# Attention's value product, one head at a time: high and low parts of the values side by side in the columns of the array

## The chip, the cores and the metric

The kernel runs on one core of a Trainium2 chip. The metric is the device time of one execution in microseconds (us). TensorE (PE in the profile; PEld is its loading of weights) multiplies matrices, VectorE (DVE) and ScalarE (ACT) work element by element, GpSimd (POOL) helps out, and SyncE (SP) issues most of the DMAs. Each engine works through its own list in order and waits where an operand or a buffer is not ready.

## What is computed

One decoder layer for 256 positions of width 1024, in float32. Cut to what matters here:

```python
proj = x @ w_in                      # q | k | v | B | C | h | gate_attn | gate_conv
y_att = moba_attention(q, k, v) @ w_attn_out       # 8 heads of 64
y_cnv = (gate_b * causal_dwconv(gate_c * h_in, conv_w_mix)) @ w_conv_out
mix = (g_att * y_att + g_cnv * y_cnv) @ w_o
x = layer_norm(ALPHA * x + mix)
u = causal_dwconv(x @ w_up);  f = (silu(u_gate) * u_val) @ w_down
x = layer_norm(ALPHA * x + f)
```

The block length of the attention is 256, so with 256 positions it is plain causal attention: for each head, `softmax(q k^T / 8, causal) @ v`.

## The kernel before

**High and low parts.** Every float32 factor `a` is split into two numbers of the type that TensorE reads here (F32R): `h`, a copy rounded to it by ScalarE, and `l = a - h`, by VectorE. A product then takes three passes, high by high, high by low and low by high; the fourth, low by low, is left out. `mm3` (lines 305 to 307) writes the three passes one after the other; `hl_split` (219, 220) and `low` (216) make the parts.

**Weights.** They come from memory in chunks of two units (128 x 1024 each), in three raw buffers. `split_h` (192) and `split_l` (197) make `wh` and `wl` of a unit. The DMA that refills a raw buffer waits on SyncE's queue until `split_l` has read what was in it.

**Slots.** After the products for q, k and v the kernel goes through the weight units one after the other; a unit is a slot. C0 is the first unit after q, k and v, and slot n below means unit C0+n. Slots 0 to 11 are the short convolution's products, slots 12 to 27 the 16 gate products (g0 to g15, slot 12+j for gj), and from slot 28 on come the products `y` of the mixed stage, which read the attention's result `aT`. What else is to be done is written into the slots by hand, with `at(slot, part, function)`. In each slot the instructions are issued in this order: the slot's weight product and then its "pe" entries on TensorE; its "act" entries and then `split_h` of the unit 5 slots ahead on ScalarE; `split_l` of the unit 4 slots ahead and then its "dve" entries on VectorE. Entries of one slot stand in the order of registration: attention pair 0 to 3 first, then the convolution, then the gates.

**Gate products.** `cols_pair` issues 8 products 512 wide (323) for each unit and, at the second unit of a pair, 16 products 256 wide (330) for both. Their sum lies in two halves of a PSUM bank; two slots later ScalarE copies one half (639) and VectorE adds the other (643, `gs`). There are four such banks, so product g(j+4) can start only when `gs` number j is done. `gate` (646) is the sigmoid; it stands one slot after its `gs` and reads it.

**Attention, by pairs of heads.** In slots 4 to 13 the scores, the masks and the exponentials are done. What follows for pair p:

- `normalize` (418, 422) on VectorE, `probs_T` (428 to 430) on TensorE: six transposes of 128 x 128 into two PSUM banks, one per head;
- `probs_h` (434) and `probs_l` (216), one slot later for the first head and two slots later for the second: the transposed probabilities' parts, into `PT` (in the profile `vpt`, which holds the values as well);
- `attend`: six products into one PSUM bank, with the values of both heads (128 columns) as weights and both heads' queries side by side in the bank (512 wide for the keys 0 to 127, 256 wide for the keys 128 to 255);
- `attend_h` (451) and `attend_l` (216): from each head's columns in the bank its 64 rows are kept, the rest is dropped, and `aT`'s high and low part are made from them, one head at a time.

The banks of scores, transposes and `attend` come from a pool of four that is used in turn. The slots of these steps are in the last `for` of the diff, as `(masked, exps, normalize, probs_T, attend)` for each pair.

Of the kernel before, what the change touches and what calls it, by code (L numbers as in the profile page):

```python
# [12 lines left out]
AF = mybir.ActivationFunctionType  # L13
ALU = mybir.AluOpType

P = 128
S = 256
# [3 lines left out]
HD = 64  # L21
# [116 lines left out]
def layer_kernel(ctx: ExitStack, tc: tile.TileContext, x, wpack, cpack, ln1_g, ln1_b, ln2_g, ln2_b, out):  # L138
    nc = tc.nc
# [10 lines left out]
    def acc_bank(name):  # L150
        return psum.tile([P, 512], F32, tag="acc", name=name)

    def ps_bank(name):
        return ps_pool.tile([P, 512], F32, tag="ps", name=name)

    def scratch(shape, name, bufs=None, tag="scr"):
        return tmp.tile(shape, F32, tag=tag, name=name, bufs=bufs or 6)
# [57 lines left out]
    def low(l, src, h):  # L215
        nc.vector.tensor_tensor(l, src, h.bitcast(F32), op=ALU.subtract)

    def hl_split(h, l, src, eng=None):
        nc.scalar.activation(h, src, AF.Copy)  # L219
        (eng or nc.vector).tensor_tensor(l, src, h.bitcast(F32), op=ALU.subtract)  # L220
# [82 lines left out]
    def mm3(o, ah, al, bh, bl, start, stop):  # L303

        nc.tensor.matmul(o, ah, bh, start=start, stop=False)  # L305
        nc.tensor.matmul(o, ah, bl, start=False, stop=False)  # L306
        nc.tensor.matmul(o, al, bh, start=False, stop=stop)  # L307
# [34 lines left out]
    qk = big.tile([P, 2, 2, AW], F32, tag="rows", name="qk")  # L342
    qkT = big.tile([P, 2, KT, S], F32R, tag="b16", name="qkT")
    vpt = big.tile([P, 3584], F32R, tag="c16", name="vpt")
    vp = vpt[:, 0:2048].rearrange("p (a t n) -> p a t n", a=2, t=2)
    PT = vpt[:, 2048:3584].rearrange("p (a j n) -> p a j n", a=2, j=2)
    aT = big.tile([P, 4, 2, S], F32R, tag="d8", name="aT")
    yT = big.tile([P, 4, 2, S], F32R, tag="e8", name="yT")
# [30 lines left out]
    SB, SM, PR = {}, {}, {}  # L379
# [58 lines left out]

    def attend(p):

        b = ps_bank(f"av{p}")
        vs = slice(p * P, (p + 1) * P)
        mm3(b, vp[:, 0, 0, vs], vp[:, 1, 0, vs], PT[:, 0, :, 128:384], PT[:, 1, :, 128:384], True, False)
        late = b.rearrange("p (j q) -> p j q", j=2)[:, :, 128:256]
        mm3(late, vp[:, 0, 1, vs], vp[:, 1, 1, vs], PT[:, 0, :, 0:128], PT[:, 1, :, 0:128], False, True)
        PR[p, "o"] = b

    def attend_h(p):
        for j in range(2):
            hs = slice(j * HD, (j + 1) * HD)  # L450
            nc.scalar.activation(aT[hs, p, 0, :], PR[p, "o"][hs, j * 256:(j + 1) * 256], AF.Copy)

    def attend_l(p):
        for j in range(2):
            hs = slice(j * HD, (j + 1) * HD)
            low(aT[hs, p, 1, :], PR[p, "o"][hs, j * 256:(j + 1) * 256], aT[hs, p, 0, :])

# [2 lines left out]
    def at(u, part, f, *a):  # L462
        beside.setdefault(u, {}).setdefault(part, []).append((f, a))
# [29 lines left out]

    def evac_v(banks):
        for t in range(2):
            hl_split(vp[:, 0, t], vp[:, 1, t], banks[t])

    C0 = U[(OFF_H, 0)]
    for t in range(2):
# [5 lines left out]

    at(C0 + 4, "pe", scores, (0, 1))
    at(C0 + 9, "pe", scores, (2, 3))
    for p, (m, e, n, tr, av) in enumerate(((5, 6, 8, 11, 14), (7, 8, 14, 15, 18), (10, 11, 17, 19, 22), (12, 13, 21, 23, 26))):
        at(C0 + m, "dve", masked, p)
        at(C0 + e, "act", exps, p)  # L510
        at(C0 + n, "dve", normalize, p)
        at(C0 + tr, "pe", probs_T, p)
        for j in range(2):
            at(C0 + tr + 1 + j, "act", probs_h, p, j)
            at(C0 + tr + 1 + j, "dve", probs_l, p, j)
        at(C0 + av, "pe", attend, p)
        at(C0 + av + 1, "act", attend_h, p)
        at(C0 + av + 1, "dve", attend_l, p)


    def x_split(k):
# [18 lines left out]
    banks = [[acc_bank(f"{m}{t}") for t in range(2)] for m in "qk"] + [[ps_bank(f"v{t}") for t in range(2)]]  # L540
# [24 lines left out]
    for k in range(1, KT):  # L565
        for m in range(3):
            if k >= KT - 2 and m < 2:
                split(C0 + 2 * (k - KT + 2) + m)
            qkv_passes(k, m, (0, 1), (0, 1, 2))
            if k == KT - 1:  # L570
                if m < 2:
                    evac_rows(m, banks[m])
                else:
                    evac_v(banks[m])
        qkv_split(k + 2)
        if 2 <= k <= 4:
            rope_tables(k - 2)
# [199 lines left out]
    banks = [acc_bank(f"o0{nh}") for nh in range(2)]  # L777
# [6 lines left out]
    banks = [acc_bank(f"o1{nh}") for nh in range(2)]  # L784
# [136 lines left out]
    for c in range(1, NP // 2):  # L921
        for e in range(2):
# [3 lines left out]
            d = i - 3  # L926
# [122 lines left out]
```

## Time and profile before

| what | value |
|---|---|
| time, median of 3 runs | 366.98 us (366.85 to 367.76) |
| profiled execution, its own time | 369.54 us |
| span of the profiled execution | 367.6 us |
| busy, PE / PEld | 357.9 / 309.7 us |
| busy, DVE / ACT / POOL | 296.9 / 222.9 / 12.9 us |
| gate products and attention's second part (slots 12 to 27) | about 80 to 131 us of the span |

Times in the profile are counted from the start of the span. A row of the timeline gives the start, the duration, engine, line, operation, what is written and read, and, in brackets, how long the engine had been idle before and what ended that. A row of the chain of waits gives the start, the time up to the next link and what ran. The durations of products are modelled ends; how fast they follow one another is read from their starts.

### The profile page before, as it was taken

How to read it: one execution, taken by the hardware profiler on the slowest of the kernel's cores; microseconds unless marked ns; L12 is line 12 of the kernel's file. 1: busy time of each engine (PE TensorE's matmuls, PEld its weight loads, DVE VectorE, ACT ScalarE, POOL GpSimd, SP SyncE). 2: the span in 40 equal slices, each digit the busy share in tenths (PEclk: the TensorE clock that was granted, in tenths of full speed). 3: DMA queues.
4: the chain of work that ended last, by engine and by line, in shares of the span. 5: the costliest groups of instructions: out<-in, count | busy, mean ns of one | idle time of the engine just before them, and what ended most of it. 6: DMA issues, size and time to landing. Idle time of an engine off the chain costs nothing.

```text
span 367.6 us, 5212 instructions
## 1 busy us (share of the span) xinstructions
PE 357.9 (97%) x1958; PEld 309.7 (84%) x1958; DVE 296.9 (81%) x510; ACT 222.9 (61%) x380; POOL 12.9 (3%) x34
## 2 busy tenths in 40 slices
PE   7999999999999999999999999999999999999991
PEld 6888888889888888888888888888888888888891
DVE  4795697779887669989769798879778697999784
ACT  4773866666976676654276665756757476686300
POOL 2000000000000002301000000000000000000000
PEclk9999999999999999999999999999999999999998
DMA  8988363524836543597250827356280726662011
GB/s 268 351 305 341 116 231 134 210 114 130 329 123 221 179 166 114 201 335 261 119 211 27 306 111 261 116 229 227 118 339 28 318 77 269 230 233 111 2 57 57
DMA packets 11240, 69.61 MB, mean 189 GB/s; under 512 B 1232, under 2 KB 1616, under 8 KB 4176
## 3 DMA queue, kind: packets, MB, share of 16 engines
q1 hardware_dynamic: 10496, 67.00, 49.3%
q0 software_dynamic: 576, 2.10, 1.8%
q8 instruction: 15, 0.25, 0.3%
q10 hardware_dynamic: 144, 0.20, 0.1%
q14 instruction: 9, 0.07, 0.1%
HBM read 68.24 MB, written 1.05 MB: 189 GB/s over the span
## 4 chain that ended last, share of the span: by engine, by line
PE 96%; DVE 1%; DMA 1%; DVEq 0%; SPq 0%; issue 0%
PE pb L323 20%; PE pb L330 10%; PE g L323 8%; PE d L305 5%; PE d L306 5%; PE d L307 5%; PE g L330 4%; PE y L323 4%; PE q L546 3%; PE k L546 3%; PE v L546 3%; PE b L323 2%; PE y L330 2%; PE c L323 2%; PE o L307 2%; PE h L323 2%
## 5 line engine op out<-in xcount | busy, mean ns | idle before, releaser
L197 DVE TENSOR_TENSOR wl<-raw,wh 128x1024 fp32r<-128x1024 f32 x99 | 121.2, 1226 | 27.2 <-ACT wh L192 26.6
L192 ACT ACTIVATE wh<-raw 128x1024 fp32r<-128x1024 f32 x99 | 103.7, 1054 | 32.5 <-DMA raw<-in_wpack 32.4
L323 PE MATMUL pb<-x1T,wh 128*128 128x512 f32 x320 | 76.2, 390 | 0.0
L323 PEld LDWEIGHTS pb<-x1T,wh 128*128 128x128 f32 x320 | 59.7, 188 | 12.2
L330 PEld LDWEIGHTS pb<-x1T,wl 128*128 128x128 f32 x320 | 41.0, 191 | 1.6
L330 PE MATMUL pb<-x1T,wl 128*128 128x256 f32 x320 | 41.5, 283 | 0.0
L220 DVE TENSOR_TENSOR wl<-raw,wh 128x1024 fp32r<-128x1024 f32 (+1 forms) x29 | 27.2, 982 | 9.6 <-ACT wh L219 9.3
L323 PE MATMUL g<-xT,wh 128*128 128x512 f32 x128 | 31.7, 394 | 0.0
L305 PE MATMUL d<-wh,f 128*128 128x512 f32 x80 | 31.3, 391 | 0.0
L306 PE MATMUL d<-wl,f 128*128 128x512 f32 x80 | 31.3, 391 | 0.0
L307 PE MATMUL d<-wh,f 128*128 128x512 f32 x80 | 31.1, 389 | 0.0
L219 ACT ACTIVATE wh<-raw 128x1024 fp32r<-128x1024 f32 (+1 forms) x29 | 23.7, 859 | 10.4 <-DMA raw<-in_wpack 6.2
L323 PEld LDWEIGHTS g<-xT,wh 128*128 128x128 f32 x128 | 23.2, 188 | 4.4
L835 DVE SCALAR_TENSOR_TENSOR fc<-fb,consts,fc 128x254 f32<-128x254 f32 x40 | 19.3, 483 | 1.4
L827 ACT ACTIVATE fc<-fb,consts 128x256 f32<-128x256 f32 x40 | 18.0, 497 | 2.0 <-DVE fb L821 2.0
L833 DVE SCALAR_TENSOR_TENSOR fc<-fb,consts,fc 128x255 f32<-128x255 f32 x40 | 19.1, 478 | 0.0
L817 ACT ACTIVATE fb<-pb 128x512 f32<-128x512 f32 x20 | 11.8, 591 | 9.8 <-PE pb L330 9.8
L307 PEld LDWEIGHTS d<-wh,f 128*128 128x128 f32 x80 | 15.0, 188 | 3.2
L305 PEld LDWEIGHTS d<-wh,f 128*128 128x128 f32 x80 | 15.1, 189 | 2.7
L306 PEld LDWEIGHTS d<-wl,f 128*128 128x128 f32 x80 | 15.1, 188 | 2.6
L330 PEld LDWEIGHTS g<-xT,wl 128*128 128x128 f32 x128 | 16.4, 191 | 0.6
L330 PE MATMUL g<-xT,wl 128*128 128x256 f32 x128 | 16.6, 283 | 0.0
(181 smaller groups left out, 577.7 us busy)
## 6 DMA issues: line engine op xcount, KB each, us to landing
raw<-in_wpack SPq DMA_DIRECT2D x55, 1024.0 KB, 5.0
raw<-in_wpack SPq DMA_DIRECT2D x6, 896.0 KB, 5.7
xr<-in_x SPq DMA_DIRECT2D x1, 1024.0 KB, 7.1
ln<-in_ln_g POOLq DMA_DIRECT2D x2, 512.0 KB, 5.3
ln<-in_ln_b POOLq DMA_DIRECT2D x2, 512.0 KB, 5.9
raw<-in_wpack SPq DMA_DIRECT2D x3, 256.0 KB, 3.8
raw<-in_wpack SPq DMA_DIRECT2D x1, 512.0 KB, 5.9
out<-x SPq DMA_DIRECT2D x2, 256.0 KB, 2.0
```

What stands on the lines that cost most here:

```text
L192: nc.scalar.activation(units[u]["h"], raw_of(u), AF.Copy)
L197: nc.vector.tensor_tensor(units[u]["l"], raw_of(u), units[u]["h"].bitcast(F32), op=ALU.subtract)
L219: nc.scalar.activation(h, src, AF.Copy)
L220: (eng or nc.vector).tensor_tensor(l, src, h.bitcast(F32), op=ALU.subtract)
L305: nc.tensor.matmul(o, ah, bh, start=start, stop=False)
L306: nc.tensor.matmul(o, ah, bl, start=False, stop=False)
L307: nc.tensor.matmul(o, al, bh, start=False, stop=stop)
L323: nc.tensor.matmul(bank, un["h"][:, k, n0:n0 + P], b[:, k].rearrange("p a s -> p (a s)"), start=k == 0, stop=False)
L330: nc.tensor.matmul(bank[:, 0:S], un["l"][:, k, n0:n0 + P], b[:, k, 0], start=False, stop=k == nk - 1)
L546: nc.tensor.matmul(banks[m][t], (xl if p == 2 else xh)[:, k, t * P:(t + 1) * P], wl if p == 1 else wh, start=k == 0 and p == 0, stop=k == ...
L833: nc.vector.scalar_tensor_tensor(c[:, 1:S], pb[:, a * S:a * S + S - 1], w_ffn(1, j), c[:, 1:S], op0=ALU.mult, op1=ALU.add)
L835: nc.vector.scalar_tensor_tensor(c[:, 2:S], pb[:, a * S:a * S + S - 2], w_ffn(0, j), c[:, 2:S], op0=ALU.mult, op1=ALU.add)
```

## The change

The values `vp` are laid out anew: for each pair of heads 256 columns, namely the first head's high and low part and the second head's low and high part, 64 columns each. `attend` now takes one head at a time: its weights are the 128 columns of that head (high and low part), and the moving operand is the high and the low part of that head's probabilities side by side (2 x 256 queries for the keys 0 to 127, 2 x 128 for the rest). So there are four products per pair in place of six, in two PSUM banks in place of one. Each bank holds all four cross products of its head in separate corners, and three of them must be added: `attend_out` copies two corners to SBUF with ScalarE (four copies of 64 rows per pair) and adds them on GpSimd, `attend_sum` adds the third on VectorE out of PSUM, and `attend_hl` splits the sum into `aT`'s two parts. The second step of the split on ScalarE thus comes behind `split_h` of its slot and behind VectorE's sum. Pairs 2 and 3 have some slots moved one earlier.

```diff
-    vp = vpt[:, 0:2048].rearrange("p (a t n) -> p a t n", a=2, t=2)
+    vp = vpt[:, 0:2048].rearrange("p (t g n) -> p t g n", t=2, g=4)
...
     def attend(p):
-        b = ps_bank(f"av{p}")
-        vs = slice(p * P, (p + 1) * P)
-        mm3(b, vp[:, 0, 0, vs], vp[:, 1, 0, vs], PT[:, 0, :, 128:384], PT[:, 1, :, 128:384], True, False)
-        late = b.rearrange("p (j q) -> p j q", j=2)[:, :, 128:256]
-        mm3(late, vp[:, 0, 1, vs], vp[:, 1, 1, vs], PT[:, 0, :, 0:128], PT[:, 1, :, 0:128], False, True)
-        PR[p, "o"] = b
-
-    def attend_h(p):
+        PR[p, "o"] = [ps_bank(f"av{p}_{j}") for j in range(2)]
+        for j in range(2):
+            b = PR[p, "o"][j]
+            js = slice(j * P, (j + 1) * P)
+            nc.tensor.matmul(b, vp[:, 0, p, js], PT[:, :, j, 128:384], start=True, stop=False)
+            nc.tensor.matmul(b.rearrange("p (a q) -> p a q", a=2)[:, :, 128:256], vp[:, 1, p, js], PT[:, :, j, 0:128],
+                             start=False, stop=True)
+
+    def attend_out(p):
+        c = PR[p, "c"] = scratch([P, 2, S], f"ac{p}")
+        for j in range(2):
+            b, hs, ls = PR[p, "o"][j], slice(j * HD, (j + 1) * HD), slice((1 - j) * HD, (2 - j) * HD)
+            nc.scalar.activation(c[hs, 0], b[hs, S:2 * S], AF.Copy)
+            nc.scalar.activation(c[hs, 1], b[ls, 0:S], AF.Copy)
+        nc.gpsimd.tensor_tensor(c[:, 0], c[:, 0], c[:, 1], op=ALU.add)
+
+    def attend_sum(p):
+        c = PR[p, "c"]
         for j in range(2):
             hs = slice(j * HD, (j + 1) * HD)
-            nc.scalar.activation(aT[hs, p, 0, :], PR[p, "o"][hs, j * 256:(j + 1) * 256], AF.Copy)
-
-    def attend_l(p):
-        for j in range(2):
-            hs = slice(j * HD, (j + 1) * HD)
-            low(aT[hs, p, 1, :], PR[p, "o"][hs, j * 256:(j + 1) * 256], aT[hs, p, 0, :])
+            nc.vector.tensor_tensor(c[hs, 0], PR[p, "o"][j][hs, 0:S], c[hs, 0], op=ALU.add)
+
+    def attend_hl(p):
+        hl_split(aT[:, p, 0, :], aT[:, p, 1, :], PR[p, "c"][:, 0])
...
     def evac_v(banks):
         for t in range(2):
-            hl_split(vp[:, 0, t], vp[:, 1, t], banks[t])
+            b = banks[t].rearrange("p (g j d) -> p g j d", g=4, j=2)
+            o = vp[:, t].rearrange("p g (a d) -> p g a d", d=HD)
+            hl_split(o[:, :, 0:4:3], o[:, :, 1:3], b)
...
-    for p, (m, e, n, tr, av) in enumerate(((5, 6, 8, 11, 14), (7, 8, 14, 15, 18), (10, 11, 17, 19, 22), (12, 13, 21, 23, 26))):
+    for p, (m, e, n, tr, av) in enumerate(((5, 6, 8, 11, 14), (7, 8, 14, 15, 18), (10, 11, 17, 18, 21), (12, 13, 20, 22, 25))):
...
         at(C0 + av, "pe", attend, p)
-        at(C0 + av + 1, "act", attend_h, p)
-        at(C0 + av + 1, "dve", attend_l, p)
+        at(C0 + av + 1, "act", attend_out, p)
+        at(C0 + av + 2, "dve", attend_sum, p)
+        at(C0 + av + 2, "dve", attend_hl, p)
```

## The prediction

> **What bounds the kernel now.** I read the busy times first, then the shares of the chain that ended last, then that chain in order of time from 40 us on, where the attention lies.
>
> ```profile
> PE 357.9 (97%) x1958; PEld 309.7 (84%) x1958; DVE 296.9 (81%) x510; ACT 222.9 (61%) x380; POOL 12.9 (3%) x34
> ...
> PE 96%; DVE 1%; DMA 1%; DVEq 0%; SPq 0%; issue 0%
> ...
> 87.16 0.23 PE av L305
> 87.39 0.23 PE av L306
> 87.61 0.23 PE av L307
> 87.84 0.11 PE av L305
> 87.95 0.12 PE av L306
> 88.07 0.12 PE av L307
> 88.19 1.84 PE g L323 x8
> ...
> 98.19 1.84 PE g L323 x8
> ...
> 111.03 1.84 PE g L323 x8
> ...
> 130.53 0.93 PE y L323 x4
> ...
> 131.93 0.93 PE y L323 x4
> ```
>
> TensorE carries 96% of the chain, and between the rows shown here link follows link with no other engine between them. So a product less is time less, as long as no new wait opens on TensorE, and a new wait counts in full. How near VectorE and ScalarE are to opening one, the busy times of the stage tell (columns: stretch, length, then PE, PEld, DVE, ACT, POOL busy, clock, DMA):
>
> ```profile
> 80.00:105.00 25.00, 25.00 (x149) 22.14 (x148) 22.82 (x51) 19.35 (x40) 0.00 (x0) 1.00 0.51 184
> 105.00:131.00 26.00, 26.00 (x154) 23.02 (x153) 18.56 (x32) 19.02 (x36) 0.00 (x0) 1.00 0.52 188
> ```
>
> From 80 to 105 us VectorE is busy for 22.82 of 25 us. There is little room for more work, and none for waiting.
>
> **What TensorE saves.** The six products of a pair take 88.19 - 87.16 = 1.03 us, 0.23 for one 512 wide and 0.115 for one 256 wide. Two of each are left: 0.69. The four pairs save 4 x 0.34 = 1.37 us. That is the whole possible gain; it would bring 366.98 to 365.6.
>
> **What the others pay.** The rows of slots 15 to 17, with those that price the new operations:
>
> ```profile
> 88.23 0.77 ACT L451 ACTIVATE aT<-av 64x256 fp32r<-64x256 f32 x2 [1.54 <-PE av L307]
> 89.02 0.39 ACT L639 ACTIVATE gs<-g 128x256 f32<-128x256 f32 x1
> 89.30 1.05 ACT L192 ACTIVATE wh<-raw 128x1024 fp32r<-128x1024 f32 x1
> 89.85 0.86 DVE L216 TENSOR_TENSOR aT<-av,aT 64x256 fp32r<-64x256 f32 x2
> 90.74 0.42 DVE L643 TENSOR_TENSOR gs<-g,gs 128x256 f32<-128x256 f32 x1
> 91.08 1.22 DVE L197 TENSOR_TENSOR wl<-raw,wh 128x1024 fp32r<-128x1024 f32 x1
> 92.37 0.49 ACT L434 ACTIVATE vpt<-ptp 128x384 fp32r<-128x384 f32 x1 [2.01 <-PE ptp L430]
> 92.76 0.90 ACT L602 ACTIVATE ct<-z,consts 128x256 f32<-128x256 f32 x2
> 92.89 0.56 DVE L216 TENSOR_TENSOR vpt<-ptp,vpt 128x384 fp32r<-128x384 f32 x1 [0.59 <-ACT vpt L434]
> 93.37 1.91 DVE L608 SCALAR_TENSOR_TENSOR ct<-z,consts,ct 128x256 f32<-128x256 f32 x4
> 93.56 0.37 ACT L639 ACTIVATE gs<-g 128x256 f32<-128x256 f32 x1
> 93.82 1.05 ACT L192 ACTIVATE wh<-raw 128x1024 fp32r<-128x1024 f32 x1
> 95.20 0.42 DVE L643 TENSOR_TENSOR gs<-g,gs 128x256 f32<-128x256 f32 x1
> 95.53 1.22 DVE L197 TENSOR_TENSOR wl<-raw,wh 128x1024 fp32r<-128x1024 f32 x1
> 97.33 1.01 DVE L422 TENSOR_SCALAR sm<-sm,st 128x128 f32<-128x128 f32 x4
> 98.26 0.42 DVE L643 TENSOR_TENSOR gs<-g,gs 128x256 f32<-128x256 f32 x1
> 99.00 0.49 ACT L646 ACTIVATE gates<-gs,consts 128x256 f32<-128x256 f32 x1
> 106.90 0.42 DVE L643 TENSOR_TENSOR gs<-g,gs 128x256 f32<-128x256 f32 x1
> 115.69 0.43 DVE L643 TENSOR_TENSOR gs<-g,gs 128x256 f32<-128x256 f32 x1
> 135.51 0.74 POOL L693 TENSOR_TENSOR m<-m 128x256 f32<-128x256 f32 x1 [132.92 <-DVE m L692]
> 136.66 0.41 ACT L696 ACTIVATE mT<-m 128x256 fp32r<-128x256 f32 x1
> 136.97 1.05 ACT L192 ACTIVATE wh<-raw 128x1024 fp32r<-128x1024 f32 x1
> 139.14 0.42 DVE L216 TENSOR_TENSOR mT<-m,mT 128x256 fp32r<-128x256 f32 x1
> ```
>
> Full-height operations overlap the next: a `gs` of 0.42 is followed after 0.34 (90.74 to 91.08). The half-height ones do not: two on ScalarE take from 88.23 to 89.02, 0.40 each, and two on VectorE from 89.85 to 90.74, 0.44 each. So ScalarE pays, per pair, four copies at 0.40 and one split at 0.31 (136.66 to 136.97) in place of two at 0.40: +1.1 us. VectorE pays two sums at about 0.43 and one `low` at 0.34 in place of two lows at 0.44: +0.3 us. GpSimd's addition, 0.74, has a slot to itself and is hidden.
>
> The Trainium skill, "ScalarE: Activation LUTs", section "What ACT_TABLE_LOAD costs", has back-to-back ACTIVATEs overlap by about 93 ns, and gives 186 ns + 0.833 ns per element with immediate scale; by that a copy of 256 elements would advance the queue by an estimated 0.31 us, and the sum below would come out at about -0.25 us instead of +0.5. The full-height rows agree with the overlap (89.02 to 89.30), the half-height pair does not, and I go by the pair.
>
> **What the new order costs.** The larger price is a wait. `attend_hl`'s split on ScalarE stands behind `split_h` of its slot, and VectorE's `low` waits for it with all its later work behind it. I carried the lists of slots 14 to 35 forward by the durations above: an operation starts when its engine is free and its operands are there, 0.03 to 0.05 us after they end (92.37 + 0.49 = 92.86, read at 92.89). On the kernel before this gives `gs` 6 at 106.91 and `gs` 9 at 115.71, where the rows have 106.90 and 115.69, the first y product at 130.55 against 130.53, and no wait on TensorE. On the kernel after:
>
> Slot 16: TensorE is 0.34 earlier. ScalarE: `probs_h` 91.97, the two tap copies, `gs` copy, `wh` 93.43 to 94.48, and only then the split of pair 0, 94.38 to 94.79. VectorE has its sums done at 92.50, and idles 2.33 us until 94.84. Behind that stand `probs_l`, four taps and `gs` 2, which starts at 97.48 instead of 95.20. TensorE wants that bank for g6 at 97.85 and waits 0.09 us.
>
> Slots 17 to 19: VectorE, late by 2.3, finishes the normalization of pair 2 at 100.58 and starts `gs` 3 at 100.55 (98.26 before). ScalarE's sigmoid 3 waits for it until 101.01 (99.00 before), and then come the four copies of pair 1, 102.63 to 104.22, `probs_h`, and `wh` until 106.35. The transposes of pair 2, now in slot 18, start at 100.47, just behind what they read and behind `probs_l` of pair 1 (99.50), which frees their banks.
>
> Slot 20 has, on VectorE, the sums, the split, `probs_l` of pair 2, the normalization of pair 3 and the convolution's low part, after 0.85 us more of waiting for ScalarE's split (108.78, behind `wh`). `gs` 6 starts at 111.78 and ends at 112.20. Before it started at 106.90, against 111.03 for the product that needs it: a reserve of 3.7 us. Now TensorE is ready for g10 at 111.16 and waits 1.08 us.
>
> Slots 21 to 25: sigmoid 6 waits for that `gs`, and the four copies of pair 2 follow it; `gs` 9 starts at 120.52 (115.69 before), and TensorE waits for it 0.65 us before g13, from 120.34 on.
>
> Slots 26 to 28: the copies of pair 3 start at 125.13 and `aT` is complete at 131.39. The y products start at 131.02 with the convolution's share, 1.4 us (130.53 to 131.93 before the change), and come to `aT` at 132.42: no wait, with 1.0 us of reserve. The y stage then runs on with its own waits unchanged.
>
> Sum: waits of 0.09 + 1.08 + 0.65 = 1.82, less 1.37 saved: +0.45 us. The profiled execution would go from 369.54 to about 370.0; it lies 2.6 us above the median, which I take as common to both. The median: 366.98 + 0.45 = 367.4 us.
>
> **Priced at nothing.** The new layout's copies have as many elements as before, and nothing reads them until the first av product near 87 us. The split lows that free raw buffers come up to 4.3 us later; the refill takes 5.0 us to land and is wanted five slots on, so with about 5 us of reserve.
>
> ```profile
> raw<-in_wpack SPq DMA_DIRECT2D x55, 1024.0 KB, 5.0
> ```
>
> **Bounds.** With copies that overlap (0.27 each) the walk gives -0.6 us; with 0.40, +0.45; with a delay of 0.08 us at each handover, +0.8.
>
> **Rivals.** (1) The gain arrives whole: 366.98 - 1.37 = 365.6. It needs VectorE's 2.3 us in slot 16 to go unfelt. For it speaks the reserve of 3.7 us at slot 22; against it, that the delay is not made up in a stage where VectorE is busy 22.82 of 25 us, and that slot 20 got more work. Chance 0.10. (2) Slower: the copies across the halves. Two of four copies per pair read rows 64 to 127 and write rows 0 to 63, or the other way round, and no row of the trace shows such a copy. If they take longer, ScalarE's queue is later by that much at each pair, and both long waits of TensorE grow with it: at 0.55 us on average the walk gives waits of 3.0 and +1.7, so 368.6. It turns into a loss that can be measured from 0.48 us on. Any other cost that keeps ScalarE as much longer acts alike. Chance 0.30. (3) The forecast, between the two, at -0.6 to +1.0: 366.4 to 368.0. Chance 0.60.
>
> **Numbers.** About 0.3%, 1.1 us, is what a measurement of this kernel can tell from no change. Faster by more: 0.10, from the first rival. Within: 0.60. Slower by more: 0.30. The range, 366.2 to 368.9, leaves out the first rival and the upper third of the second.
>
> **What would show it.** The av products take 0.69 per pair in the chain. VectorE's longest idle time in this stage is about 2.3 us near 92.5, before `aT`'s low, released by ScalarE's split. TensorE waits for VectorE's `gs` near 111 and near 120, about 1.1 and 0.7 us. `aT` is done before the y products ask for it. The forecast is wrong if no wait of g on `gs` appears (then the first rival), if the copies last over 0.48 us (the second), or if y waits for `aT`.

## The result, and the profile after

The changed kernel takes 368.64 us (median of 6 runs, 368.48 to 368.90), the kernel before 367.22 us beside it (366.71 to 367.76). The ratio is 1.0034, with a 95% interval of 1.0021 to 1.0047: slower by 1.25 us (0.77 to 1.73).

The page of the changed kernel, busy times and shares of the chain; line numbers above 344 are shifted against the kernel before (by one up to `attend`; VectorE's `gs`, 643 before, is 657 here):

```profile
PE 355.7 (97%) x1950; PEld 306.5 (84%) x1950; DVE 297.6 (81%) x514; ACT 226.5 (62%) x392; POOL 16.4 (4%) x38
...
PE 89%; DVE 4%; ACT 4%; issue 1%; DMA 1%; DVEq 0%; SPq 0%; ACTq 0%
```

TensorE is busy for 2.2 us less. But its part of the chain fell from 96% to 89%, and ScalarE and VectorE are now in it with 4% each (before, VectorE had 1% and ScalarE was not listed). Where they enter, the chain in order of time shows:

```profile
84.81 0.23 PE av L447
...
85.50 1.86 PE g L323 x8
...
91.26 0.95 ACT wh L192
92.20 0.31 ACT aT L219
...
92.54 0.43 DVE aT L220
...
118.56 0.34 DVE gs L657
...
119.04 2.08 PE g L323 x8
```

The four products of a pair take 85.50 - 84.81 = 0.69 us, as counted. From about 90 to 119 us the chain then runs through ScalarE's weight split, its split of pair 0's sum behind it, VectorE's `low` behind that and the `gs` behind all of it; TensorE takes it over again only at 119.04; between 89.61 and there the chain has no product in it. The table of waits names the place where it begins, with four waits of 4.3 us in all, the longest 2.4:

```profile
DVE aT L220 <- ACT aT L219: 4.3, 4, 2.4
```

**How long the stage is.** The whole spans of two executions can't be set against each other here. The profiled execution of before lost 2.35 us ahead of the stage (g2 starts at 85.16 there and at 82.81 here), 0.97 of it while waiting for the first piece of memory, 3.62 against 2.65 us in the two chains. So I measure from the first product of g2 (slot 14) to the first one of y (slot 28), in the timeline of TensorE. The kernel before, first and last row:

```profile
85.16 2.00 PE L323 MATMUL g<-xT,wh 128*128 128x512 f32 x8
...
130.37 1.09 PE L323 MATMUL y<-yT,wh 128*128 128x512 f32 x4
```

That is 45.21 us. The changed kernel:

```profile
82.81 2.00 PE L323 MATMUL g<-xT,wh 128*128 128x512 f32 x8
...
89.69 3.92 PE L323 MATMUL g<-xT,wh 128*128 128x512 f32 x16
...
95.85 2.09 PE L323 MATMUL g<-xT,wh 128*128 128x512 f32 x8 [0.33 <-DVE gs L657]
...
99.04 2.10 PE L323 MATMUL g<-xT,wh 128*128 128x512 f32 x8
...
102.89 3.82 PE L323 MATMUL g<-xT,wh 128*128 128x512 f32 x16
...
110.17 2.09 PE L323 MATMUL g<-xT,wh 128*128 128x512 f32 x8 [0.84 <-DVE gs L657]
...
112.67 2.09 PE L323 MATMUL g<-xT,wh 128*128 128x512 f32 x8
...
116.51 2.00 PE L323 MATMUL g<-xT,wh 128*128 128x512 f32 x8
...
119.04 2.08 PE L323 MATMUL g<-xT,wh 128*128 128x512 f32 x8 [0.52 <-DVE gs L657]
...
123.58 3.80 PE L323 MATMUL g<-xT,wh 128*128 128x512 f32 x16
...
129.12 1.09 PE L323 MATMUL y<-yT,wh 128*128 128x512 f32 x4
```

46.31 us, 1.10 more. Three products wait for `gs`: g6 at 95.85, g10 at 110.17 and g13 at 119.04. The stage accounts for 1.10 of the 1.25 us, and the rest lies within the interval.

### The profile page after: what moved, and what is told of

The parts are those of the page before. It is cut to its first block, busy times and chain, and to the rows that moved or that the text cites. A ratio compares the mean times of both kernels' runs of the same rounds, so it can differ in the third digit from the quotient of the medians.

```text
span 366.4 us, 5218 instructions
## 1 busy us (share of the span) xinstructions
PE 355.7 (97%) x1950; PEld 306.5 (84%) x1950; DVE 297.6 (81%) x514; ACT 226.5 (62%) x392; POOL 16.4 (4%) x38
## 4 chain that ended last, share of the span: by engine, by line
PE 89%; DVE 4%; ACT 4%; issue 1%; DMA 1%; DVEq 0%; SPq 0%; ACTq 0%
PE pb L323 20%; PE pb L330 10%; PE d L305 5%; PE d L306 5%; PE d L307 5%; PE y L323 4%; PE g L323 4%; PE q L560 3%; PE k L560 3%; PE v L560 3%; PE b L323 2%; PE g L330 2%; PE y L330 2%; PE c L323 2%; PE o L306 2%; PE o L305 2%
```

## The experiments

Two theories stood against each other. **Order**: VectorE stands still because ScalarE's high part of `aT` is queued behind the weight split of its slot. **Work**: the four copies of ScalarE and the additional sums fill the queues, wherever they stand. Times are given as ratios to the kernel before, measured beside each.

**e1, the order mended.** Only the place of the last step changes (`attend_high` and `attend_low` are the two lines of `attend_hl`):

```diff
-        at(C0 + av + 2, "dve", attend_hl, p)
+        if p < 3:
+            at(C0 + av + 3, "act", attend_high, p)
+            at(C0 + av + 3, "dve", attend_low, p)
+        else:
+            at(C0 + av + 2, "dve", attend_hl, p)
```

> The changed kernel with one thing moved: for pairs 0 to 2 the split of the sum goes one slot later, its high part into ScalarE's entries ahead of the weight split, its low part into VectorE's entries of that slot. No operation more or less. Order theory (VectorE stands still because ScalarE's high part is queued behind the weight split): no wait of g on gs is left on TensorE, VectorE's idle time of 2.4 us ahead of aT's low is gone, and the whole saving of the products comes through: 1.36 us below the kernel before, about 365.9. Work theory (ScalarE's four copies a pair and VectorE's sums fill the queues): the same operations cost the same, so the waits near 110 and 119 us stay and the time stays 1 us or more above the kernel before.

Measured: 0.9966 (0.9953 to 0.9978), 1.25 us faster than the kernel before, 366.15 against 367.46 us. VectorE's rows of slots 16 and 17:

```profile
90.18 0.56 DVE L216 TENSOR_TENSOR vpt<-ptp,vpt 128x384 fp32r<-128x384 f32 x1
...
92.49 0.42 DVE L667 TENSOR_TENSOR gs<-g,gs 128x256 f32<-128x256 f32 x1
...
93.95 0.42 DVE L216 TENSOR_TENSOR aT<-ac,aT 128x256 fp32r<-128x256 f32 x1
```

`probs_l` is no longer held up (90.18; the `low` ahead of it had started at 92.54), `gs` 2 starts 2.8 us earlier (92.49 against 95.28), and `low` comes a slot later without idle time ahead of it. TensorE's rows:

```profile
82.76 2.00 PE L323 MATMUL g<-xT,wh 128*128 128x512 f32 x8
...
89.64 3.92 PE L323 MATMUL g<-xT,wh 128*128 128x512 f32 x16
...
95.32 2.00 PE L323 MATMUL g<-xT,wh 128*128 128x512 f32 x8
...
98.42 2.10 PE L323 MATMUL g<-xT,wh 128*128 128x512 f32 x8
...
102.27 3.82 PE L323 MATMUL g<-xT,wh 128*128 128x512 f32 x16
...
108.55 1.99 PE L323 MATMUL g<-xT,wh 128*128 128x512 f32 x8
...
110.95 2.09 PE L323 MATMUL g<-xT,wh 128*128 128x512 f32 x8
...
114.80 3.82 PE L323 MATMUL g<-xT,wh 128*128 128x512 f32 x16
...
121.08 3.80 PE L323 MATMUL g<-xT,wh 128*128 128x512 f32 x16
...
126.62 1.09 PE L323 MATMUL y<-yT,wh 128*128 128x512 f32 x4
```

No wait is left; the stage takes 43.86 us, 1.35 less than before the change. The same operations in another order: the work theory falls as an explanation of the loss by itself. Two things move together here, the split's slot and its place ahead of the weight split; no run takes them apart. This version is faster than the kernel before, and than the changed kernel, whose ratio (1.0021 to 1.0047) lies wholly above this one.

**e2, the products alone.** The new products with the old evacuation and the old slots; of each bank's corners only one is used, so the attention's result lacks the other two. One line of the difference to the kernel before:

```diff
-            nc.scalar.activation(aT[hs, p, 0, :], PR[p, "o"][hs, j * 256:(j + 1) * 256], AF.Copy)
+            nc.scalar.activation(aT[hs, p, 0, :], PR[p, "o"][j][hs, 0:S], AF.Copy)
```

> The kernel before with the new layout of the values and the four products a pair, but its own evacuation (one corner of each bank, high and low part as before) and its own slots; the other two corners are left out of the sum. Both theories: TensorE's saving by itself, av at 0.69 us a pair, no wait of g on gs, 1.36 us below the kernel before, about 365.9. If the products themselves were the cost, it would not be faster.

Measured: 0.9959 (0.9946 to 0.9972), 1.5 us faster. In the trace the stage takes 43.94 us (82.30 to 126.24), 1.27 less than before, and no product waits for `gs`. The products bring what was counted, and e1 has nearly all of it.

**e3, the order alone.** The kernel before, with its last two steps moved for three pairs:

```diff
-        at(C0 + av + 1, "act", attend_h, p)
-        at(C0 + av + 1, "dve", attend_l, p)
+        if p < 3:
+            at(C0 + av + 2, "dve", attend_h, p)
+            at(C0 + av + 2, "dve", attend_l, p)
+        else:
+            at(C0 + av + 1, "act", attend_h, p)
+            at(C0 + av + 1, "dve", attend_l, p)
```

> The kernel before with only the order changed: for pairs 0 to 2 both parts of aT are made one slot later and in VectorE's part of the slot, so ScalarE's copies are queued behind the weight split. Same operations, same products. Order theory: VectorE idles about 3 us in slot 16 ahead of aT's low, TensorE waits for gs 2 before g6 (1.3 us) and a little (0.1 to 0.2 each) at g7, g10 and g11: about 2.0 us above the kernel before, about 369.2. Work theory: nothing is added, so no change, 367.2.

Measured: 1.0060 (1.0047 to 1.0074), 2.2 us slower. VectorE ahead of pair 0's low part, and TensorE's first row, the one with the wait and the last:

```profile
93.50 0.86 DVE L216 TENSOR_TENSOR aT<-av,aT 64x256 fp32r<-64x256 f32 x2 [4.14 <-ACT aT L451]
```

```profile
83.10 2.00 PE L323 MATMUL g<-xT,wh 128*128 128x512 f32 x8
...
97.26 2.08 PE L323 MATMUL g<-xT,wh 128*128 128x512 f32 x8 [1.13 <-DVE gs L647]
...
130.27 1.09 PE L323 MATMUL y<-yT,wh 128*128 128x512 f32 x4
```

The stage takes 47.17 us, 1.96 more than before. Nothing was added; the order by itself costs more than the products save. VectorE idles longer here than expected (4.14 us where about 3 had been expected) and longer than in the changed kernel (2.40), so e3 shows that such an order costs time, and not how much of the changed kernel's loss it is; for that stands e1.

**e4, less work, the same order.** The changed kernel without two of a pair's four copies and without GpSimd's addition; the sum lacks the corner low by high.

```diff
-            nc.scalar.activation(c[hs, 1], b[ls, 0:S], AF.Copy)
-        nc.gpsimd.tensor_tensor(c[:, 0], c[:, 0], c[:, 1], op=ALU.add)
```

> The changed kernel without the corner low by high: two of the four copies of each pair and GpSimd's addition are left out, the order stays. ScalarE has 0.78 us less to do a pair. Order theory: VectorE's stand in slot 16 is as long as before, the waits of TensorE at g6 (0.5) and partly g10 (0.3) stay, the later one goes: 0.4 us below the kernel before, about 366.8. Work theory (the copies are the cost): no wait left, 1.36 us below, about 365.9.

Measured: 1.0002 (0.9990 to 1.0014). The time is not told apart from that of the kernel before. The interval reaches from 0.37 us faster to 0.51 us slower: the 1.36 us of the work theory are excluded, and the 0.4 of the order theory lies at its edge.

```profile
92.75 0.42 DVE L220 TENSOR_TENSOR aT<-ac,aT 128x256 fp32r<-128x256 f32 x1 [2.70 <-ACT aT L219]
```

```profile
83.01 2.00 PE L323 MATMUL g<-xT,wh 128*128 128x512 f32 x8
...
96.05 2.08 PE L323 MATMUL g<-xT,wh 128*128 128x512 f32 x8 [0.33 <-DVE gs L655]
...
127.87 1.09 PE L323 MATMUL y<-yT,wh 128*128 128x512 f32 x4
```

VectorE stands still no less than in the changed kernel, 2.70 us against 2.40, and the wait at g6 stays as it was (0.33 idle in both). The stage is 44.86 us, 0.35 less than in the kernel before, so close to the 0.4 of the order theory. Half of the copies gone is worth 1.45 us of the stage, though, because the later waits shrink: with the order wrong, work adds to the delay. Either remedy takes the loss away; the order is the larger part, 46.31 - 43.86 = 2.45 us of the stage in e1.

**e5, the order mended for pair 0 alone** (`if p < 1` in the diff of e1).

> The changed kernel with the order mended for pair 0 alone (high part one slot later, ahead of the weight split); pairs 1 to 3 stay as changed. If the delay of slot 16 is carried on from slot to slot: the wait at g6 (0.5 us) is gone, the one at g10 shrinks from 1.1 to 0.2, the one at g13 (0.7, made by pair 2 and slot 23's own work) stays: stage 0.3 us shorter than in the kernel before, about 367.1. If each pair makes its own wait: the waits at g10 and g13 stay whole, about 0.6 us longer than the kernel before, about 368.1.

Measured: 0.9975 (0.9961 to 0.9990), 0.9 us faster than the kernel before.

```profile
83.11 2.00 PE L323 MATMUL g<-xT,wh 128*128 128x512 f32 x8
...
115.14 4.13 PE L323 MATMUL g<-xT,wh 128*128 128x512 f32 x16
...
121.73 3.80 PE L323 MATMUL g<-xT,wh 128*128 128x512 f32 x16
...
127.28 1.09 PE L323 MATMUL y<-yT,wh 128*128 128x512 f32 x4
```

The stage is 44.17 us, 1.04 less than before. From g12 to g14 it takes 121.73 - 115.14 = 6.59 us, where e1 takes 6.28 (114.80 to 121.08), so 0.3 is left there (0.7 had been expected) and nothing elsewhere. The delay of slot 16 was carried on, more of it than I had expected: with pair 0 alone mended, 2.1 of the 2.4 us that were lost come back.

**e6, slot 20 relieved.** In the changed kernel, the slot of pair 3's normalization:

```diff
-(12, 13, 20, 22, 25)
+(12, 13, 21, 22, 25)
```

> The changed kernel with the normalization of pair 3 moved back from slot 20 to slot 21 and nothing else. If slot 20's wait is the pile of VectorE's work in that one slot (1.1 us for the normalization): the wait at g10 goes, those at g6 (0.5) and g13 (0.6) stay, and the time falls by 1.1 us to that of the kernel before, about 367.4. If the order alone counts, the wait at g10 stays and the time stays at about 368.6.

Measured: 1.0016 (0.9999 to 1.0034). The median is 367.81 us, between the two expectations, and the time leaves it open whether this differs from the kernel before; the trace is clearer:

```profile
84.15 2.00 PE L323 MATMUL g<-xT,wh 128*128 128x512 f32 x8
...
104.22 3.82 PE L323 MATMUL g<-xT,wh 128*128 128x512 f32 x16
...
110.50 1.98 PE L323 MATMUL g<-xT,wh 128*128 128x512 f32 x8
...
129.37 1.09 PE L323 MATMUL y<-yT,wh 128*128 128x512 f32 x4
```

From g8 to g10 it takes 6.28 us, as in e1 (102.27 to 108.55) and not 7.28 as in the changed kernel: the wait at g10 is gone. The stage is 45.22 us, 1.09 less than in the changed kernel and as long as in the kernel before. So the largest wait needed both, the delay from slot 16 and the normalization moved into slot 20.

**e7, the copies twice**, in the kernel e1:

```diff
-            nc.scalar.activation(c[hs, 0], b[hs, S:2 * S], AF.Copy)
-            nc.scalar.activation(c[hs, 1], b[ls, 0:S], AF.Copy)
+            for _ in range(2):
+                nc.scalar.activation(c[hs, 0], b[hs, S:2 * S], AF.Copy)
+                nc.scalar.activation(c[hs, 1], b[ls, 0:S], AF.Copy)
```

> The kernel with the order mended for pairs 0 to 2, and each of the four copies of a pair made twice: 1.6 us more of ScalarE a pair, nothing else. If the mended order has made ScalarE's work free of cost: still about 366.1. If what is left of reserve is smaller than 1.6 us a pair: waits come back at g9 (0.4), g10 (0.6) and g13 (1.3) and two small ones at the start of the y stage (0.9 together), in all about 2.3 us above the kernel before, 369.7.

Measured: 1.0097 (1.0068 to 1.0126), 3.6 us slower than the kernel before.

```profile
121.05 2.06 PE L323 MATMUL g<-xT,wh 128*128 128x512 f32 x8 [1.31 <-DVE gs L668]
...
132.58 1.15 PE L323 MATMUL y<-yT,wh 128*128 128x512 f32 x4 [1.29 <-DVE ac L465]
```

The mended order has not made ScalarE's work free: 1.6 us more a pair is beyond its reserve. By the starts of the products, set against e1, TensorE loses 0.46 us at g9, 0.64 at g10 and 1.47 at g13, where 0.4, 0.6 and 1.3 were expected. The y products now wait 1.29 us for pair 3's sum, where I had expected 0.9 in that place. The stage takes 48.08 us (84.50 to 132.58), 2.87 more than before; the 3.6 us, above the 2.3 expected, have an interval of 2.5 to 4.6.

## Why the prediction was right or wrong

The time lies in the range, 366.2 to 368.9. The likeliest case does not hold: it said +0.45 us, and +1.25 (0.77 to 1.73) was measured, just beyond the 0.3% (1.1 us) within which I had put six chances in ten, though the interval reaches back into it. That the time is still in the range is due to the room left for the second rival, whose reason did not come true. The mechanism was the one described, as e1 and e3 show from both sides; its size was off.

**What held.** av at 0.69 us per pair. VectorE's stand ahead of pair 0's `low`: 2.33 expected, 2.40 measured. The places of the three waits. Moved by the 2.35 us that the execution of before was later, `gs` 6 was expected at 109.43 and `gs` 9 at 118.17; they start at 109.61 and 118.48:

```profile
95.28 0.42 DVE L657 TENSOR_TENSOR gs<-g,gs 128x256 f32<-128x256 f32 x1
...
109.61 0.42 DVE L657 TENSOR_TENSOR gs<-g,gs 128x256 f32<-128x256 f32 x1
...
118.48 0.41 DVE L657 TENSOR_TENSOR gs<-g,gs 128x256 f32<-128x256 f32 x1
...
129.31 0.43 DVE L220 TENSOR_TENSOR aT<-ac,aT 128x256 fp32r<-128x256 f32 x1 [0.55 <-ACT aT L219]
```

`aT` is complete at 129.74, and y reads it first at 130.53, 0.8 us later (1.0 expected). GpSimd's addition stays hidden.

**What failed: the term "waits of 0.09 + 1.08 + 0.65 = 1.82".** With e1, which has the same products in the same slots and no wait, each one can be measured. From g4 to g6: 6.16 us (89.69 to 95.85) against 5.68, so 0.48. From g8 to g10: 7.28 against 6.28, so 1.00. At g13, 119.04 - 116.51 = 2.53 against the 1.84 of eight products, so 0.69. And each time the products behind the wait take longer: g6 to g7 3.19 against 3.10, g10 to g11 2.50 against 2.40, g13 to g14 4.54 against 4.44. In all 2.17 + 0.29 = 2.46, less 1.37 saved: +1.09, and the stage shows +1.10.

The three waits are not separate bills. Between 89.61 and 119.04 the chain holds no product, so g13 starts when `gs` 9 lets it, however long TensorE stood at g6 and g10: the wait at g6, 0.39 longer than forecast, put TensorE back and left less to wait at g10, 1.00 against 1.08. The sum is therefore checked at g13, and four things were missing there, 0.66 us together; the stage lies 46.31 - 45.21 - 0.45 = 0.65 above the forecast.

VectorE was late: `gs` 2, expected at 97.48 - 2.35 = 95.13, starts at 95.28, and `gs` 9 ends at 118.89 where 118.17 + 0.42 = 118.59 was expected, 0.30 later. The handover from VectorE to TensorE is not 0.03 to 0.05 us, which I had read from handovers between other engines: `gs` 2 ends at 95.70 and g6 starts at 95.85, `gs` 6 ends at 110.03 and g10 starts at 110.17, 0.14 to 0.15 us, so 0.1 more. The products behind the wait take another 0.1. And for TensorE I had taken the times of the chain, which are 0.16 us later than the starts in the timeline (88.19 against 88.03 for g3), so that it could in truth have begun earlier than I had it ready. At g6, where the forecast was only 0.09 us beyond a reserve, all this shows in full.

**The rivals.** The first, the gain arrives whole, needed the 2.3 us to go unfelt; e1 shows it true once they are gone. The second landed on the right side for the wrong reason: copies across the halves do not take longer. Both kinds of copy in the view of the tile av:

```profile
L456 ACT ACTIVATE ac<-av x8: 362/380/382, 85.2 to 124.2; 64x256 f32<-64x256 f32 x8
L457 ACT ACTIVATE ac<-av x8: 376/379/383, 85.6 to 124.6; 64x256 f32<-64x256 f32 x8
```

L456 stays in its rows and L457 changes the half, at 380 and 379 ns. In the timeline they follow one another after 0.37 to 0.40 us, so my 0.40 by the half-height pair was nearly right. The 0.31 us that I had estimated from the Trainium skill, "ScalarE: Activation LUTs", section "What ACT_TABLE_LOAD costs", which measured tiles of 128 rows, does not carry over to these copies of 64 rows.

**The profiled execution** of before lay 2.6 us above the median, and I took that as common to both kernels. It was not: the changed kernel's profiled execution has 368.48 us, beside a median of 368.64.

## What to carry to other kernels

Where a step has one half on ScalarE and the other on VectorE, look at its place in both lists as well as at its cost; here the place weighed more. A short operation behind a long one on the first engine stopped everything queued on the second, and the delay was carried on to the next place without reserve; moving three such splits by a slot turned a loss of 1.25 us into a gain of 1.25. Before an operation is moved, compare for each product what releases it and how much earlier that was: 3.7 us here at g10, used up by a delay, a heavier slot and an earlier product together.

## What I had not expected of the hardware

A wait of TensorE costs more than the wait: 0.14 to 0.15 us from the end of VectorE's operation to the first product's start, and 0.09 to 0.10 us more for the products behind it. Counted at each of the three waits, that is about 0.7 of the 2.46 us; by the chain only the share at g13 set the time. Half-height copies of ScalarE whose rows change from one to the next do not overlap here, 0.37 to 0.40 us each, while the full-height copies of as many elements per row for `gs` (653) advance the queue by 0.26 to 0.28 us. Whether the height or the change of rows does it, no run here separates.
